# One moving operand of 512 columns for the experts' gate and up matmuls, with the halves added outside TensorE

## The chip, the cores and the metric

The kernel runs on one core of one Trainium2 chip. The metric is the device time of one execution in microseconds. Beside the times there is one profiled execution, and all rows below come from its trace. A core has five engines that run side by side, each through its own queue in order: TensorE (PE in the rows; its weight loads are shown apart as PEld), VectorE (DVE), ScalarE (ACT), GpSimd (POOL) and SyncE (SP), which here only issues transfers.

## The reference

The reference is one block of a diffusion transformer over 2048 tokens of 1024 features: a modulated layer norm, a projection, a gated convolution branch, a retention branch in both directions, a mixing projection, a layer norm, and then a mixture of experts in which each of 16 experts takes its own 256 tokens. The part that matters here is the last:

```
aff = softmax(h @ w_router);  gates, idx = top_k(aff.T, 256)      # per expert
xe  = h[idx]                                                      # 256 x 1024 per expert
he  = silu(xe @ w_gate[e]) * (xe @ w_up[e])                       # 256 x 1024
ye  = (he @ w_down[e]) * gates                                    # 256 x 1024
out = layer_norm(alpha * x + g2 * scatter_add(ye, idx)) * ln2_g + ln2_b
```

## The kernel before, in words

All matrix products run in TensorE's reduced float32 type. To keep float32 accuracy, each operand is split into a high part (the value copied into that type) and a low part (the value minus the high part). A product is then three matmuls into one PSUM bank: high by high, high by low, low by high. The helper `split` (lines 78 to 84) makes the two parts: ScalarE writes the high part (line 80) and VectorE subtracts for the low part (line 81). The helper `mm3` (lines 86 to 89) issues the three matmuls, so lines 87, 88 and 89 stand for all of them in the rows, and lines 80 and 81 for all splits; the tile names tell them apart.

The experts are the loop at line 1160. Per expert:

- `x_gather` (line 1094) fetches the 256 token rows of the next expert by an indirect transfer. `x_prep` (line 1104) transposes them on TensorE and splits them into `xeT`, a tile of 8 blocks of 128 features, in each block first 256 columns of high parts and then 256 of low parts (one column per token).
- Gate and up (lines 1171 to 1181): four steps `f2`, each making two blocks `fb` of 128 hidden features. The weights come in as float32 (`rg`, a ring of 4 buffers, issued by SP) and are split into `sg` tiles (a ring of 24 buffers under the tag `w`, shared with all other split weights and with the row tiles of the end). The weights are the stationary operand, the tokens the moving one. For a block, 8 feature blocks times `mm3` accumulate 256 columns of the gate, then the same for up. One PSUM bank (`pg`) holds the gate of both blocks, one (`pu`) up of both. Then ScalarE applies Silu from the gate's bank (line 1179), VectorE multiplies by the up bank (line 1180), and the product is split into `heT` (line 1181).
- Down (lines 1191 to 1235): two halves `n` of the output features, each 8 steps times two token tiles of `mm3` with 512 moving columns of split `w_down` (`sd`), collected by line 1211 and added into the rows of `d_acc` in memory by an indirect transfer.

PSUM banks for matmuls come from two tags with two buffers each, taken in turn (`mm_ps`, lines 66 to 70), so four banks go round.

The order of the work on each engine is set when the program is built, by a list scheduler that takes instructions by priority (the order of the code) and by its own idea of when they are ready. A block under `issue_after` is held back behind an instruction that it names. The final layer norm of rows is done by `finish` (line 1137), a generator: one step fetches a row tile of 128 tokens, one step `lag` steps later takes its mean and variance and starts the scaling, and the step after that ends it and writes the rows out. `pump` (line 358) runs a given number of such steps at a place in the program. From expert 11 (`FIN`) on, all 16 tiles are finished from `d_acc` as it stands (`fx` tiles); after experts 13 and 14 four tiles each are done again with what the last experts changed (`zr` tiles); the tuple `STEPS` says how many steps are run behind each part of the last two experts. The last expert's own two tiles are finished at the end.

Two small tiles `pad0` and `pad1` (line 951) only move what is allocated behind them. `pad0` has 56 words (224 bytes), after which `heT` starts on a multiple of 128 bytes in its partition. `pad1` has 8 words (32 bytes), after which both `xeT` buffers start 32 bytes past a multiple of 128. The other moving operands of the program (`hT`, the split weights, `SS`) start on a multiple of 128.

Of the kernel before, what the change touches and what calls it, by code (L numbers as in the profile page):

```python
# [20 lines left out]
P = 128  # L21
D = 1024
KD = 8
# [19 lines left out]
def body(ctx: ExitStack, tc: tile.TileContext, x, ctxt, cc, w_ada0, w_ada, b_row, b_col, w_in, conv_w, conv_b,  # L43
# [878 lines left out]
    def e2k(name):  # L922
        return ep.tile([P, 512], F32, name=name, tag="e2k", bufs=6)
# [24 lines left out]
    same, low = ksel[:, 0], ksel[:, 1]  # L948
    wg2 = []
    for i, (tag, bufs) in enumerate((("heT", 1), ("xeT", 2))):  # L950
        V.memset(ep.tile([P, (56, 8)[i]], F32, name=f"pad{i}"), 0.0)
        wg2.append(ep.tile([P, 4, D], F32, name="wg2", tag=tag, bufs=bufs))
        nc.sync.dma_start(wg2[i], w_ada[3, i * 4:i * 4 + 4].rearrange("k p f -> p k f"))
    g2fill = [ada_rows(rep_c(ep)[0], 2, 1, lambda name: e4k(name, [P, 512]), wg2)]
# [197 lines left out]
            yield  # L1152

    FIN = 11
    STEPS = ((1, 1, 1, 1, 1, 0), (1, 1, 1, 2, 1, 0))
    efill = []
    nxt = x_prep(0, x_gather(0))
    make_lists(0)
# [1 line left out]
    for e in range(NE):  # L1160
# [9 lines left out]
        heT = ep.tile([P, KD, 2, 256], F32R, name="heT", tag="heT", bufs=1)  # L1170
        for f2 in range(4):
            wg, wu = first[f2] if e == 0 and f2 < 3 else [gu_slabs(w[e], f2) for w in (w_gate, w_up)]
            pg, pu = mm_ps(), mm_ps()
            for fb in range(2):
                for w, dst in ((wg, pg), (wu, pu)):
                    for k in range(KD):
                        mm3(dst[:, fb * 256:(fb + 1) * 256], w[fb][k], (xeT[:, k, 0], xeT[:, k, 1]), k == 0, k == KD - 1)
            s = e2k("s")
            A.activation(s, pg, AF.Silu)
            evicted = V.tensor_tensor(s, s, pu, ALU.mult)  # L1180
            split(heT[:, f2 * 2:f2 * 2 + 2, 0], heT[:, f2 * 2:f2 * 2 + 2, 1], s.rearrange("p (f c) -> p f c", f=2))
            if f2 == 1 and 1 <= e < 4:
                make_lists(e)
            if f2 == 1 and e + 1 < NE:
                nxt = x_prep(e + 1, xes)
            with tc.issue_after(evicted.ins):
                if e >= NE - 2:
                    pump(STEPS[e - NE + 2][f2], efill)
                elif f2:
                    pump(1 + (f2 == 1), efill)  # L1190
# [45 lines left out]
        if e in (NE - 3, NE - 2):  # L1236

            with tc.issue_after(evicted.ins):
                pump(1000, efill)
                lo = FIN if e == NE - 3 else NE - 3  # L1240
                efill.append(finish(range(lo * 2, lo * 2 + 4), acc_rows, put_rows, 3))
                pump(3 if e == NE - 3 else 2, efill)
        for t in range(2):
            g = e * 2 + t
# [71 lines left out]
```

## Time and profile before

| what | us |
|---|---|
| median of 3 runs | 3033.33 (3030.34 to 3039.99) |
| profiled execution, its own time | 3036.01 |
| its span, first to last instruction | 3034.2 |
| TensorE busy in the span | 2942.8 |
| first gate matmul of expert 0 | 1915.1 |
| one expert in the middle (4 to 12) | 68.3 to 68.4 |
| last down matmul to the end of the span | 14.4 |

The span is read in stages. Everything ahead of the experts takes the first 1915 us; the 16 experts take the rest but for the 14 us at the end. A matmul's row gives the time from its start to its modelled end, and neighbours overlap: what a stream costs is read from start to start. The same holds for VectorE and ScalarE, where the next instruction may start some 0.08 to 0.1 us ahead of the end that a row gives.

### The profile page before, as it was taken

The numbers are of one execution on the slowest core, as the hardware profiler recorded it, in microseconds if no ns is written. First come the engines' busy times: TensorE is split into PE (matmuls) and PEld (weight loads), VectorE is DVE, ScalarE is ACT, GpSimd is POOL, SyncE is SP. The second block draws the span as 40 slices with busy tenths as digits, with TensorE's granted clock in tenths as the row PEclk, the third lists the DMA queues.
The fourth block names the chain that finished last, engine by engine and source line by source line (L and its number), as shares of the span: only waits on it lengthen the run. The fifth ranks groups of instructions, "written<-read, shape, count | busy, mean of one in ns | idle before, by whom it ended". The sixth has DMA issues, their size and how long they took to land.

```text
span 3034.2 us, 47285 instructions
## 1 busy us (share of the span) xinstructions
PE 2942.8 (97%) x18005; PEld 2593.7 (85%) x18005; DVE 2141.6 (71%) x3926; ACT 1160.3 (38%) x2110; POOL 374.7 (12%) x325
## 2 busy tenths in 40 slices
PE   6999999999999999999999996899999999999998
PEld 5988888889888888888878883899999999999997
DVE  4366788552669986888877777666666666668887
ACT  4323223242231333544421112455555555544443
POOL 2100000000000000111101114000000000014332
PEclk9999999999999999999999998899999999999999
DMA  7244345342452334666754445566677776778875
GB/s 252 88 141 174 135 165 183 111 133 93 172 185 81 129 113 143 220 209 209 232 202 153 148 140 185 193 206 210 207 221 219 215 223 214 221 239 279 289 246 205
DMA packets 194853, 559.94 MB, mean 185 GB/s; under 512 B 29017, under 2 KB 44281, under 8 KB 194625
## 3 DMA queue, kind: packets, MB, share of 16 engines
q1 hardware_dynamic: 170080, 486.60, 48.1%
q0 software_dynamic: 18064, 64.62, 7.5%
q10 hardware_dynamic: 6480, 5.70, 0.6%
q8 instruction: 141, 2.31, 0.3%
q14 instruction: 88, 0.71, 0.1%
HBM read 428.95 MB, written 127.89 MB: 184 GB/s over the span
## 4 chain that ended last, share of the span: by engine, by line
PE 87%; DMA 5%; DVE 4%; ACT 2%; issue 2%; POOL 1%; POOLq 0%; SPq 0%; DVEq 0%; ACTq 0%
PE mm L87 24%; PE mm L89 24%; PE mm L88 24%; PE tr L160 2%; PE ro L87 2%; PE ro L89 2%; PE ro L88 2%; DMA rg<-w_up 1%; DVE st L140 1%; PE o L88 1%; PE o L89 1%; PE o L87 1%; DVE sg L81 1%; DMA out<-fx 1%; PE u L160 0%
## 5 line engine op out<-in xcount | busy, mean ns | idle before, releaser
L87 PE MATMUL mm<-xeT,sg 128*128 128x256 f32 x2048 | 574.1, 281 | 0.0
L89 PE MATMUL mm<-xeT,sg 128*128 128x256 f32 x2048 | 572.8, 280 | 1.2 <-DVE sg L81 1.2
L88 PE MATMUL mm<-xeT,sg 128*128 128x256 f32 x2048 | 572.5, 280 | 0.0
L81 DVE TENSOR_TENSOR sg<-rg,sg 128x512 fp32r<-128x512 f32 x488 | 329.5, 689 | 231.8 <-ACT sg L80 229.8
L80 ACT ACTIVATE sg<-rg 128x512 fp32r<-128x512 f32 x512 | 313.6, 629 | 303.1 <-PE mm L89 217.9
L89 PEld LDWEIGHTS mm<-xeT,sg 128*128 128x128 f32 x2048 | 385.6, 188 | 1.6 <-DVE sg L81 1.6
L88 PEld LDWEIGHTS mm<-xeT,sg 128*128 128x128 f32 x2048 | 385.7, 188 | 0.6
L87 PEld LDWEIGHTS mm<-xeT,sg 128*128 128x128 f32 x2048 | 385.5, 188 | 0.6
L491 DVE SCALAR_TENSOR_TENSOR cacc<-yw,cvw,cacc 128x384 f32<-128x384 f32 (+1 forms) x600 | 376.4, 640 | 8.0
L81 DVE TENSOR_TENSOR sd<-rd,sd 128x512 fp32r<-128x512 f32 x256 | 172.0, 688 | 86.8 <-ACT sd L80 86.2
L80 ACT ACTIVATE sd<-rd 128x512 fp32r<-128x512 f32 x256 | 156.9, 629 | 134.7 <-PE mm L89 82.5
L87 PE MATMUL mm<-sd,heT 128*128 128x512 f32 x512 | 199.9, 390 | 1.6 <-ACT heT L80 1.4
L89 PE MATMUL mm<-sd,heT 128*128 128x512 f32 x512 | 199.8, 390 | 0.4 <-DVE heT L81 0.4
L88 PE MATMUL mm<-sd,heT 128*128 128x512 f32 x512 | 199.5, 390 | 0.0
L154 POOL TENSOR_TENSOR rs<-rs,mhalf 128x1 f32<-128x1 f32 (+1 forms) x50 | 38.5, 770 | 1273.3 <-DVE rs L153 1272.8
L87 PE MATMUL mm<-hT,sU 128*128 128x256 f32 x512 | 147.1, 290 | 4.0 <-ACT us L732 2.2
L147 POOL TENSOR_TENSOR rs<-rs,mhalf 128x1 f32<-128x1 f32 x58 | 106.6, 1838 | 345.4 <-DVE rs L146 342.0
L88 PE MATMUL mm<-hT,sU 128*128 128x256 f32 x512 | 147.2, 288 | 0.0
L89 PE MATMUL mm<-hT,sU 128*128 128x256 f32 x512 | 146.6, 288 | 0.0
L1246 POOL DMA_INDIRECT d_acc<-ye,idx x30 | 50.1, 1670 | 567.3 <-DVE ye L1211 470.8
L468 ACT ACTIVATE gs<-mm 128x512 f32<-128x512 f32 x96 | 55.0, 597 | 163.8 <-PE mm L89 142.7
L87 PEld LDWEIGHTS mm<-sd,heT 128*128 128x128 f32 x512 | 96.2, 188 | 21.6 <-ACT heT L80 2.4
(360 smaller groups left out, 7136.4 us busy)
## 6 DMA issues: line engine op xcount, KB each, us to landing
rg<-w_gate SPq DMA_DIRECT2D x128, 512.0 KB, 4.6
rg<-w_up SPq DMA_DIRECT2D x128, 512.0 KB, 3.6
rd<-w_down SPq DMA_DIRECT2D x128, 512.0 KB, 4.3
wa<-w_ada SPq DMA_DIRECT2D x40, 512.0 KB, 4.1
d_v<-vs SPq DMA_DIRECT2D x32, 512.0 KB, 2.6
vsr<-d_v SPq DMA_DIRECT2D x32, 512.0 KB, 5.5
xt<-x SPq DMA_DIRECT2D x16, 512.0 KB, 3.6
rU<-w_in SPq DMA_DIRECT2D x16, 512.0 KB, 4.7
```

Of the source, the lines that this page charges most:

```text
L80: A.activation(hi, src, AF.Copy)
L81: eng.tensor_tensor(lo, src, hi.bitcast(F32), ALU.subtract)
L87: T.matmul(ps, s[0], m[0], start=start, stop=False)
L88: T.matmul(ps, s[0], m[1], start=False, stop=False)
L89: return T.matmul(ps, s[1], m[0], start=False, stop=stop_)
L140: V.bn_stats(st[:, i], src[:, i * w:(i + 1) * w])
L147: pows[0] = G.tensor_tensor(rs, rs, mhalf[:, :1], ALU.pow)
L154: G.tensor_tensor(rs[:, 0], rs[:, 0], mhalf[:, :heads], ALU.pow)
L160: T.transpose(ps[:, j * P:(j + 1) * P], src[:, (k0 + j) * P:(k0 + j + 1) * P], ident)
L468: A.activation(s, ps, AF.Sigmoid)
L491: V.scalar_tensor_tensor(acc[:, :n], y[:, tap:tap + n], cvw[:, cgp, tap:tap + 1], acc[:, :n], op0=ALU.mult, op1=ALU.add)
L1246: G.indirect_dma_start(out=d_acc, out_offset=bass.IndirectOffsetOnAxis(ap=idx[:, g:g + 1], axis=0), in_=yes[t], in_offset=None, compute_op ...
```

## The change

Gate and up no longer use `mm3`. For each weight block and each feature block there are now two matmuls: the high weights against the 512 columns of high and low tokens at once (line 1180 of the new file), and the low weights against the 256 columns of high tokens (line 1181), added into the first half of the same bank. A whole bank now holds one product of one block: the first half has high by high plus low by high, the second half high by low. To end it, ScalarE copies the second half out (line 1182), VectorE adds the first half to the copy (line 1183), and for the gate ScalarE applies Silu in place (line 1185). The multiplication (line 1186) and the split into `heT` are done per block, on 256 columns, where they were done per step on 512.

`pad1` is gone. The finishing generator that is started after expert 14 gets a `lag` of 2 where it had 3, and the last row of `STEPS` is changed.

```diff
     for i, (tag, bufs) in enumerate((("heT", 1), ("xeT", 2))):
-        V.memset(ep.tile([P, (56, 8)[i]], F32, name=f"pad{i}"), 0.0)
+        if i == 0:
+            V.memset(ep.tile([P, 56], F32, name="pad0"), 0.0)
...
-    STEPS = ((1, 1, 1, 1, 1, 0), (1, 1, 1, 2, 1, 0))
+    STEPS = ((1, 1, 1, 1, 1, 0), (1, 1, 2, 1, 0, 0))
...
-            pg, pu = mm_ps(), mm_ps()
             for fb in range(2):
-                for w, dst in ((wg, pg), (wu, pu)):
+                banks = mm_ps(), mm_ps()
+                s = e2k("s")
+                parts = s[:, 0:256], s[:, 256:512]
+                for w, ps, part in zip((wg, wu), banks, parts):
                     for k in range(KD):
-                        mm3(dst[:, fb * 256:(fb + 1) * 256], w[fb][k], (xeT[:, k, 0], xeT[:, k, 1]), k == 0, k == KD - 1)
-            s = e2k("s")
-            A.activation(s, pg, AF.Silu)
-            evicted = V.tensor_tensor(s, s, pu, ALU.mult)
-            split(heT[:, f2 * 2:f2 * 2 + 2, 0], heT[:, f2 * 2:f2 * 2 + 2, 1], s.rearrange("p (f c) -> p f c", f=2))
+                        T.matmul(ps, w[fb][k][0], xeT[:, k].rearrange("p a c -> p (a c)"), start=k == 0, stop=False)
+                        T.matmul(ps[:, 0:256], w[fb][k][1], xeT[:, k, 0], start=False, stop=k == KD - 1)
+                    A.activation(part, ps[:, 256:512], AF.Copy)
+                    V.tensor_tensor(part, part, ps[:, 0:256], ALU.add)
+                    if ps is banks[0]:
+                        A.activation(part, part, AF.Silu)
+                evicted = V.tensor_tensor(parts[0], parts[0], parts[1], ALU.mult)
+                split(heT[:, f2 * 2 + fb, 0], heT[:, f2 * 2 + fb, 1], parts[0])
...
-                efill.append(finish(range(lo * 2, lo * 2 + 4), acc_rows, put_rows, 3))
+                efill.append(finish(range(lo * 2, lo * 2 + 4), acc_rows, put_rows, 3 if e == NE - 3 else 2))
```

ScalarE's queue in an expert in the middle, before, around the end of one step `f2` (`mm` is the gate's bank, `sg` and `sd` are split weights, numbers are buffers):

```order
L80 ACTIVATE sg_23479<-rg_23477 128x512
L80 ACTIVATE sg_23482<-rg_23477 128x512
L80 ACTIVATE sg_23487<-rg_23485 128x512
L1179 ACTIVATE s_23161<-mm_23063 128x512
L80 ACTIVATE sg_23490<-rg_23485 128x512
L80 ACTIVATE sg_23495<-rg_23493 128x512
L80 ACTIVATE sg_23498<-rg_23493 128x512
L80 ACTIVATE heT_23030<-s_23161 128x2x256
```

And now, for one block `fb`, half a step:

```order
L1182 ACTIVATE s_21223<-mm_21221 128x256
L80 ACTIVATE sg_21581<-rg_21576 128x512
L1185 ACTIVATE s_21223<-s_21223 128x256
L80 ACTIVATE sg_21586<-rg_21584 128x512
L1182 ACTIVATE s_21223<-mm_21222 128x256
L80 ACTIVATE sg_21589<-rg_21584 128x512
L80 ACTIVATE heT_21188<-s_21223 128x256
```

The weight splits keep their order; between each two of them now stands an instruction of 256 columns that belongs to a bank, and the Silu stands behind an addition on VectorE.

VectorE's queue at the same places, before:

```order
L81 TENSOR_TENSOR sg_23487<-rg_23485,sg_23487 128x512
L81 TENSOR_TENSOR sg_23490<-rg_23485,sg_23490 128x512
L81 TENSOR_TENSOR sg_23495<-rg_23493,sg_23495 128x512
L1180 TENSOR_TENSOR s_23161<-s_23161,mm_23064 128x512
L81 TENSOR_TENSOR sg_23498<-rg_23493,sg_23498 128x512
L81 TENSOR_TENSOR heT_23030<-s_23161,heT_23030 128x2x256
```

and now:

```order
L1183 TENSOR_TENSOR s_21223<-s_21223,mm_21221 128x256
L81 TENSOR_TENSOR sg_21581<-rg_21576,sg_21581 128x512
L81 TENSOR_TENSOR sg_21586<-rg_21584,sg_21586 128x512
L1183 TENSOR_TENSOR s_21223<-s_21223,mm_21222 128x256
L1186 TENSOR_TENSOR s_21223<-s_21223 128x256
L81 TENSOR_TENSOR sg_21589<-rg_21584,sg_21589 128x512
L81 TENSOR_TENSOR heT_21188<-s_21223,heT_21188 128x256
```

Where a step of 16 weight splits had two instructions of 512 columns, it now has eight of 256.

VectorE's queue in the last expert, at the end of gate and up and into down, before (`zr` are row tiles being finished, line 1211 collects the first half of down):

```order
L1180 TENSOR_TENSOR s_29858<-s_29858,mm_29761 128x512
L1146 SCALAR_TENSOR_TENSOR zr_29290<-zr_29290,rs1_29724,l2_26027 128x1024
L81 TENSOR_TENSOR heT_29298<-s_29858,heT_29298 128x2x256
L140 BN_STATS st_29865<-zr_29434 128x6 x2
L140 BN_STATS st_29876<-zr_29571 128x6
L143 BN_AGGR mv_29868<-st_29865 128x2
L140 BN_STATS st_29876<-zr_29571 128x6
L146 TENSOR_SCALAR rs1_29870<-mv_29868 128x1
L1151 SCALAR_TENSOR_TENSOR zr_29434<-zr_29434,mv_29868,l2_26026 128x1024
L143 BN_AGGR mv_29879<-st_29876 128x2
L1146 SCALAR_TENSOR_TENSOR zr_29434<-zr_29434,rs1_29870,l2_26027 128x1024
```

and now:

```order
L1183 TENSOR_TENSOR s_28754<-s_28754,mm_28753 128x256
L81 TENSOR_TENSOR heT_28276<-s_28711,heT_28276 128x256
L1186 TENSOR_TENSOR s_28754<-s_28754 128x256
L1147 SCALAR_TENSOR_TENSOR zr_28524<-zr_28524,rs1_28673,l2_25277 128x1024
L81 TENSOR_TENSOR heT_28276<-s_28754,heT_28276 128x256
L81 TENSOR_TENSOR sd_28822<-rd_28817,sd_28822 128x512
L81 TENSOR_TENSOR sd_28827<-rd_28825,sd_28827 128x512
```

The finishing of the last two repeated row tiles, which stood behind the last `heT`, now stands ahead of it; behind it are weight splits for down.

## Rows read from the trace of the kernel before

**Rows 1.** The page: busy us, share of the span and instructions of each engine.
```profile
PE 2942.8 (97%) x18005; PEld 2593.7 (85%) x18005; DVE 2141.6 (71%) x3926; ACT 1160.3 (38%) x2110; POOL 374.7 (12%) x325
```

**Rows 2.** Windows: busy us (instructions) per engine, TensorE's clock, DMA share, GB/s.
```profile
2469.80:2538.10 68.30, 68.30 (x497) 64.56 (x496) 43.30 (x65) 36.97 (x62) 5.14 (x4) 1.00 0.70 216
...
2743.20:2811.50 68.30, 68.30 (x497) 64.58 (x496) 57.33 (x94) 32.53 (x60) 29.34 (x22) 1.00 0.85 286
2811.50:2881.90 70.40, 68.96 (x498) 64.47 (x497) 60.38 (x100) 30.14 (x57) 25.55 (x22) 1.00 0.86 288
2881.90:2950.50 68.60, 68.60 (x498) 64.64 (x497) 56.30 (x89) 33.57 (x62) 25.39 (x17) 1.00 0.78 256
2950.50:3019.80 69.30, 67.58 (x481) 62.55 (x479) 55.98 (x91) 26.76 (x48) 18.44 (x14) 1.00 0.67 228
```

**Rows 3.** What TensorE waited for in the experts: us in total, times, longest.
```profile
PE mm L87 <- ACT heT L80: 1.4, 1, 1.4
PE mm L89 <- DVE sg L81: 1.2, 1, 1.2
PE ix L1048 <- ACT ob L1047: 1.2, 3, 0.4
PE mm L89 <- DVE heT L81: 0.4, 1, 0.4
```

**Rows 4.** Page, groups: xcount | busy us, mean ns of one | idle before.
```profile
L87 PE MATMUL mm<-xeT,sg 128*128 128x256 f32 x2048 | 574.1, 281 | 0.0
```

**Rows 5.** Timeline of TensorE, gate and up of expert 5: start us, us, what.
```profile
2299.74 0.28 PE L87 MATMUL mm<-xeT,sg 128*128 128x256 f32 x1
...
2300.09 0.28 PE L87 MATMUL mm<-xeT,sg 128*128 128x256 f32 x1
2300.09 0.19 PEld L88 LDWEIGHTS mm<-xeT,sg 128*128 128x128 f32 x1
...
2306.27 0.28 PE L89 MATMUL mm<-xeT,sg 128*128 128x256 f32 x1
```

**Rows 6.** Timeline of TensorE, down of expert 5.
```profile
2319.72 0.39 PE L88 MATMUL mm<-sd,heT 128*128 128x512 f32 x1
...
2329.92 0.39 PE L88 MATMUL mm<-sd,heT 128*128 128x512 f32 x1
```

**Rows 7.** Timeline of TensorE, the first projection.
```profile
719.78 0.28 PE L89 MATMUL mm<-hT,sU 128*128 128x256 f32 x1
...
726.98 0.28 PE L89 MATMUL mm<-hT,sU 128*128 128x256 f32 x1
```

**Rows 8.** Timeline of VectorE: four instructions of 256 columns and the next.
```profile
2074.81 0.42 DVE L1041 TENSOR_TENSOR oa<-pabf,kio 128x256 fp32r<-128x256 f32 x1
...
2076.15 0.69 DVE L81 TENSOR_TENSOR sd<-rd,sd 128x512 fp32r<-128x512 f32 x1
```

**Rows 9.** Timeline of VectorE, expert 13.
```profile
2857.00 4.29 DVE L81 TENSOR_TENSOR sd<-rd,sd 128x512 fp32r<-128x512 f32 x7
...
2867.84 0.69 DVE L81 TENSOR_TENSOR heT<-s,heT 128x512 fp32r<-128x512 f32 x1 [3.41 <-ACT heT L80]
```

**Rows 10.** Timeline of ScalarE, expert 8.
```profile
2478.38 0.60 ACT L1179 ACTIVATE s<-mm 128x512 f32<-128x512 f32 x1 [0.77 <-PE mm L89]
```

**Rows 11.** Groups by line, ScalarE with 256 columns: xcount | busy us, mean ns | idle before.
```profile
L680 ACT ACTIVATE o<-o,rs 128x256 f32<-128x256 f32 x64 | 30.9, 564 | 43.3 <-DVE rs L155 43.3
```

**Rows 12.** What ScalarE waited for from expert 11 on: us in total, times, longest.
```profile
ACT sd L80 <- DMA rd<-w_down: 34.4, 19, 4.2
...
ACT sd L80 <- DMA out<-fx: 11.1, 2, 7.5
```

**Rows 13.** Groups within 2743.2 to 2811.5 (expert 12), VectorE.
```profile
L1146 DVE SCALAR_TENSOR_TENSOR fx<-fx,rs,l 128x1024 f32<-128x1024 f32 x6 | 7.7, 1278 | 0.0
```

## Prediction

> **What bounds the kernel now.** I read the page first: TensorE is busy 97% of the span and VectorE 71% [rows 1]. A share over the whole span says little here, so the second view is the busy time in windows, one per expert [rows 2]. The reader is to see two things. In the middle (first line) TensorE is busy for all of 68.3 us and VectorE for 43.3, ScalarE for 37.0: TensorE alone sets the pace. In the last four experts VectorE is at 57.3, 60.4, 56.3 and 56.0 us, since the row tiles are finished there, and two windows are longer: 70.4 and 69.3. The third view, what TensorE waited for, has only some 4 us in all sixteen experts [rows 3]. So time can only be won by fewer or shorter matmuls, and can be lost where VectorE or ScalarE come late, which is near in the last four experts and far in the others.
>
> What a matmul costs is read in the timeline from start to start, since the 281 ns of the group [rows 4] overlap. In gate and up, 57 matmuls start between 2299.74 and 2306.27, so 56 steps of 116.6 ns [rows 5]. In down, with 512 columns, 45 steps from 2319.72 to 2329.92 are 226.7 ns each [rows 6]. In the first projection, 256 columns again, 60 steps take 7.20 us, 120.0 ns each [rows 7]. Between 256 and 512 columns lie 106.7 ns (226.7 less 120.0), which is 256 columns at the upper level of 2.4 GHz, and the granted clock is 1.00 in these windows [rows 2]. So every matmul costs its columns and something on top: 13.3 ns in down and in the first projection, 10 ns in gate and up. What differs between these places and is set by the program is where the moving tile starts: on a multiple of 128 bytes in the two with 13.3, and 32 bytes past one in gate and up.
>
> **The change, part by part.**
>
> *The matmuls.* Gate and up have 2048 triples (16 experts, 4 steps, 2 blocks, 2 weights, 8 feature blocks). A triple is 768 columns before and after; three instructions become two. Before: 3 x 116.6 = 349.9 ns. With the small pad gone, the token tile starts on a multiple of 128 like the moving tiles of rows 6 and 7, so I take their steps: 226.7 + 120.0 = 346.7 ns. That is 3.2 ns for 2048 triples: 6.6 us less. The bounds are wider. If the 10 ns of gate and up stay with both instructions, a triple is 116.6 + 106.7 + 116.6 = 339.9 ns, 20.5 us less. If the first instruction carries the 13.3 and the other columns run no better than the slowest 256-column step plus the same again, 226.7 + 124 (120.0 with the 4 ns that the rows scatter by), the triple is 351 and the change costs 2 us. I take the middle, because the rows with the tile's new placement say so in two stages.
>
> The Trainium skill has a formula for this gap in "TensorE: Matmul & The Clock Gate", section "Back-to-back issue gap": columns at 2.4 GHz plus 2.5 ns. By it one instruction less per triple would bring 2.5 x 2048 = 5.1 us; the rows show four to five times as much on top of the columns, but only the part that is not given back by the placement counts.
>
> *The eviction in the experts before 11.* Per expert VectorE loses 8 instructions of 512 columns and gains 32 of 256 (16 additions, 8 multiplications, 8 subtractions). From start to start, 512 columns take 0.60 us (seven in 4.29, less the last one's 0.69, over 6) [rows 9] and 256 take 0.335 (four in 1.34) [rows 8]. So 32 x 0.335 - 8 x 0.60 = 5.9 us more, 43.3 to 49.2 of 68. ScalarE loses 8 of 512 (0.60 each) [rows 10] and gains 32 of 256, each at most 0.56 [rows 11]: at most 13 us more, 37.0 to 50. Both stay hidden behind TensorE. What could uncover them is a bank that comes free late. Four banks go round; a bank is filled in 8 x 0.347 = 2.8 us, and three others are filled before it is needed again: 8.3 us. After the last matmul the Silu started 0.77 us later [rows 10]; with that wait, a copy of at most 0.56, an addition of 0.42 and one weight split ahead on each engine (0.63 and 0.69), a bank is free after 3.1 us. That is 5 us in hand, where before a pair had 11.2 us (four blocks of 2.8) for its eviction. Cost in these experts: nothing. The last `heT` block is first needed in the seventh of eight steps of down, 36 matmuls of 227 ns or 8.2 us on; nothing either.
>
> *The last four experts.* VectorE's busy time there is 57.3 + 60.4 + 56.3 + 56.0 = 230.0 of 276.6 us [rows 2]. The change adds 4 x 5.9 = 23.7: 253.7 us, 92%. Its idle time halves, 46.6 to about 21. A finishing instruction of 1024 columns holds its queue 1.28 us [rows 13] and the additions that free a bank stand behind such ones; ScalarE's copies stand behind weight splits that wait for rows to be written out (7.5 us once, on which VectorE then sat idle 3.41) [rows 12, 9]. Now the price. With TensorE alone, expert 13 would take 68.3 like the middle, and expert 15, which has no transposes, 384 x 0.1166 + 96 x 0.2267 = 66.6; so these windows hold 2.1 + 0.3 + 2.7 = 5.1 us of stalls today. Below, the new stalls can be nothing: the waits on writes come from the same places with the same lead. Above, VectorE sets the pace and keeps all its idle time: 23.7 us more, less the 1.7 that these experts would have won. I take 4 us more: the same waits on half the idle time.
>
> *The lag of 2 and STEPS.* The order shows that in the last expert the two-tile finishing work that stood between the last `heT` and down now stands ahead of it. It can give back at most the 2.7 us of expert 15 and lose none of its work, which is the same; a tile waits one step less for its reciprocal root from GpSimd, which is behind by then. I take 1 us. The pad's memset itself is one instruction far from any wait: nothing.
>
> **Sum.** 6.6 less for the matmuls, 4 more and 1 less at the end: 3.6 us less than the profiled execution's own 3036.0, so 3032.4. The median of the runs shown is 2.7 us below that execution, so I expect 3029.7, and say 3029. About 0.3% (9.1 us) is what a measurement of this kernel can tell from no change; the forecast is inside it.
>
> **The rivals.**
>
> *A. The smaller step on top of the columns holds for the new pair.* The stationary tiles are the same, and the 10 ns belong to gate and up in 6144 matmuls; if it is these weights and not the token tile's place that make them, the triple is 339.9 ns. Against it: both other stages have 13.3. Time: 20.5 less, 3 back at the end: 17.5 less, 3016.
>
> *B. VectorE becomes the bound in the last four experts (slower).* For it: 92% busy in a queue in strict order, with finishing instructions of 1.28 us ahead of the additions that free TensorE's banks, and only 8.3 us for a bank where it was 11.2. Against it: at 84 to 86% it cost 5 us in three windows. It decides when an addition comes more than 8.3 us after its bank's last matmul. Price 23.7 in full, less the 6.6 won on all matmuls: 17 more, 3050.
>
> *C. The eviction paces gate and up everywhere (slower).* Each gate bank now goes ScalarE, VectorE, ScalarE, and each hop stands behind a weight split. If a hop on average waits for two splits and not one, 3.1 us grow by 2.6 to 5.7, still under 8.3; only with four ahead does it break. Were it to cost 0.15 us a bank, 256 banks would be 38 us: 3065. Against it: ScalarE and VectorE have 18 us to spare per expert.
>
> *D. Weight loads are the bound.* PEld is busy 64.6 of 68.3 us in the middle [rows 2], and a third of gate and up's loads go. Then all that stands on top of the columns could vanish: a triple of 768 columns at 320 ns, 30 less, 61 us in all, 2972. Against it: a load starts with the matmul ahead of it (both at 2300.09) [rows 5], takes 0.19 us, and has 0.227 behind a matmul of 512 columns, yet that stream shows 13.3 on top too.
>
> The Trainium skill's "Perfetto Trace Analysis", section "Identifying the Most-Contended Engine", would have TensorE's headroom judged by the loads' busy share, which here is 94%; it is the page behind D, and rows 5 and 6 disagree with it for this stream.
>
> **How the numbers follow.** Chances: forecast 0.56, A 0.24, B 0.12, C 0.04, D 0.04. The forecast's own range, from bounds on stalls and scatter, is 3020 to 3038; 0.2 of it lies beyond 9.1 us faster, little beyond 9.1 slower. Faster by over 0.3%: 0.11 of the forecast's, 0.21 of A, 0.04 of D, together 0.36. Slower by over 0.3%: 0.03 of the forecast's, 0.10 of B, 0.04 of C, 0.17. Within: 0.47. The range of 8 in 10 takes in A and the lower half of B: 3010 to 3044.
>
> **What would show it.** In the changed trace, starts in gate and up should lie 227 and 120 ns apart in turn; 223 and 117 is A, much less is D. An expert in the middle should take 67.9 us with TensorE waiting for nothing; a wait of the new first matmul (line 1180) for line 1183's addition would be C in the middle and B after expert 11. VectorE should be busy near 49 us in the middle and 60 to 66 per window at the end, with TensorE's waits there 6 to 12 us in all. The forecast is wrong if the pair takes under 342 or over 350 ns, or if the last four experts together take over 282 us.

## The result, and the profile after

The changed kernel took 3059.14 us (median of 5 runs, 3052.51 to 3060.61), the kernel before 3032.82 beside it: ratio 1.0081, with an interval of 1.0065 to 1.0097. That is 26 us slower where 4 us less were forecast. The profiled execution took 3058.51, 22.5 us more than that of before. The stretch ahead of the experts is the same work in all runs of this document, but for a pad, and yet took between 1906 and 1918 us from one profiled execution to the next (one of the eighteen, a slow one at about half clock, is left out), so the rows per expert tell more than a single time: from the first gate matmul to the end of the span the changed kernel took 1145.5 us and that of before 1119.1, 26.4 more.

First where the time went. Windows of the changed kernel, one per expert; columns as in [rows 2] (length, busy us of TensorE, its loads, VectorE, ScalarE and GpSimd, then TensorE's clock, DMA share, GB/s). The first is expert 8, the others are experts 12 to 15:

```profile
2467.10:2535.50 68.40, 68.40 (x370) 58.99 (x369) 50.00 (x89) 42.48 (x86) 5.29 (x4) 1.00 0.72 216
2740.90:2809.40 68.50, 68.50 (x369) 58.86 (x368) 61.65 (x114) 34.23 (x76) 21.98 (x22) 1.00 0.79 268
2809.40:2890.00 80.60, 73.32 (x370) 62.02 (x369) 68.45 (x126) 39.69 (x86) 25.00 (x23) 0.94 0.76 258
2890.00:2967.60 77.60, 71.71 (x369) 61.11 (x368) 62.16 (x114) 40.28 (x86) 20.40 (x16) 0.93 0.74 236
2967.60:3045.60 78.00, 69.49 (x353) 58.10 (x352) 65.11 (x121) 33.91 (x74) 20.32 (x15) 0.98 0.63 206
```

An expert in the middle takes what it took; everything is lost in the last three: 236.2 us against 208.3 [rows 2], 27.9 more. (The experts started 3.9 us earlier in this execution, which is why the whole differs by 22.5; the first thirteen took 1.8 more, the tail behind the last matmul 3.2 less.) The 27.9 have two parts. TensorE's idle time there, length less busy, is 21.7 us against 3.2: 18.5 more. And it is busy for 214.5 us with matmuls that took 205.1: 9.4 more, at a granted clock of 0.94, 0.93 and 0.98 where it was 1.00.

What TensorE waited for from expert 12 on (us in total, times, longest), against [rows 3]:

```profile
PE mm L1180 <- DVE s L1183: 11.6, 4, 3.7
PE mm L1180 <- ACT sg L80: 5.9, 1, 5.9
PE mm L87 <- DVE s L1183: 2.8, 2, 2.0
```

The first and third are the new addition (line 1183), which frees a bank. The second is a wait for a weight split on ScalarE; it comes third in time below.

Each long wait costs twice. The clock in expert 13, in stretches around two such waits:

```profile
2838.00:2842.00 4.00, 4.00 (x25) 3.48 (x24) 1.64 (x4) 0.49 (x2) 0.00 (x0) 1.00 1.01 400
2842.00:2845.50 3.50, 0.80 (x5) 0.43 (x4) 1.41 (x3) 2.23 (x5) 0.00 (x0) 1.00 1.02 410
2845.50:2852.30 6.80, 5.49 (x16) 4.31 (x16) 6.80 (x12) 5.51 (x13) 0.55 (x1) 0.50 0.61 224
2852.30:2855.70 3.40, 0.27 (x1) 0.27 (x2) 3.34 (x9) 1.16 (x3) 1.47 (x1) 1.00 0.38 154
2855.70:2859.10 3.40, 3.40 (x12) 2.85 (x12) 3.40 (x7) 2.39 (x7) 1.36 (x2) 0.50 0.29 118
```

and TensorE's own rows behind the first:

```profile
2846.46 0.80 PE L1180 MATMUL mm<-xeT,sg 128*128 128x512 f32 x1 [3.66 <-DVE s L1183]
...
2847.27 0.63 PE L1180 MATMUL mm<-xeT,sg 128*128 128x512 f32 x1
...
2847.91 0.63 PE L1180 MATMUL mm<-xeT,sg 128*128 128x512 f32 x1
```

TensorE idled for 3.66 us up to 2846.46. Near the end of that wait the clock fell to 0.50 (1.2 and not 2.4 GHz), and a pair took 0.64 us where it takes 0.35. Near 2852.3 it rose again, while TensorE idled for the second time (3.47 us, up to 2855.43), and fell once more for 3.4 us behind that wait. The wait of 1.4 us that the kernel before had in expert 13 left the clock at 1.00 [rows 2, 3].

Why the addition was late both times, in VectorE's rows:

```profile
2842.87 1.29 DVE L81 TENSOR_TENSOR sg<-rg,sg 128x512 fp32r<-128x512 f32 x2 [3.23 <-ACT sg L80]
2845.39 0.69 DVE L81 TENSOR_TENSOR sg<-rg,sg 128x512 fp32r<-128x512 f32 x1 [1.22 <-ACT sg L80]
2845.99 0.41 DVE L1183 TENSOR_TENSOR s<-s,mm 128x256 f32<-128x256 f32 x1
...
2849.99 1.28 DVE L1147 SCALAR_TENSOR_TENSOR fx<-fx,rs,l 128x1024 f32<-128x1024 f32 x1
2851.19 1.87 DVE L140 BATCH_NORM_STATS2 st<-fx 128x6 f32<-128x512 f32 x3
...
2855.01 0.37 DVE L1183 TENSOR_TENSOR s<-s,mm 128x256 f32<-128x256 f32 x1
```

The first addition stands behind three weight splits, which wait for ScalarE's half of the split. ScalarE in turn waited for a slab that had not landed:

```profile
2842.21 1.15 ACT L80 ACTIVATE sg<-rg 128x512 fp32r<-128x512 f32 x2 [3.71 <-DMA rg<-w_up]
```

Why that slab came late no run settles. The second addition, at 2855.01, stands behind 5 us of row finishing. The third long wait, in expert 14, is of yet another kind. VectorE's finishing instruction itself waits for GpSimd's root. The next addition and the multiplication stand behind it, ScalarE's copy into `heT` waits for the multiplication, and the weight splits that TensorE needs next stand behind that copy:

```profile
2903.87 1.28 DVE L1147 SCALAR_TENSOR_TENSOR fx<-fx,rs,l 128x1024 f32<-128x1024 f32 x1 [4.31 <-POOL rs L147]
2905.07 0.41 DVE L1183 TENSOR_TENSOR s<-s,mm 128x256 f32<-128x256 f32 x1
...
2906.04 0.42 ACT L80 ACTIVATE heT<-s 128x256 fp32r<-128x256 f32 x1 [7.26 <-DVE s L1186]
...
2907.30 0.80 PE L1180 MATMUL mm<-xeT,sg 128*128 128x512 f32 x1 [5.89 <-ACT sg L80]
```

This is no wait for a bank: TensorE had filled four blocks of expert 14, and the first of their banks had been freed by an addition at 2897.66. So there are three blockers (a late slab, a row being finished, GpSimd's root) and two ways to TensorE, both through a queue in strict order: the addition that frees its bank stands behind something that is waiting or long, or its next weights stand behind an eviction that does.

Now the matmuls. TensorE's timeline in expert 6, first a stretch ahead of the transposes of the next expert's tokens, then one behind them; between the two rows of each lie 30 pairs:

```profile
2336.73 0.40 PE L1180 MATMUL mm<-xeT,sg 128*128 128x512 f32 x1
...
2347.33 0.40 PE L1180 MATMUL mm<-xeT,sg 128*128 128x512 f32 x1
...
2356.81 0.39 PE L1180 MATMUL mm<-xeT,sg 128*128 128x512 f32 x1
...
2367.21 0.39 PE L1180 MATMUL mm<-xeT,sg 128*128 128x512 f32 x1
```

A pair takes 353.3 ns in the first stretch and 346.7 in the second. Both stretches read the same token tile in the same shapes. Most experts have one of each kind, 350.0 in the mean, which is the triple of before; experts 3, 7 and 9 have 353.2 throughout. The change wins nothing on matmuls here.

### The profile page after: what moved, and what is told of

Read it like the earlier page. It is cut to its first block, busy times and chain, and to the rows that moved or that the text cites. A ratio compares the mean times of both kernels' runs of the same rounds, so it can differ in the third digit from the quotient of the medians.

```text
span 3056.7 us, 43677 instructions
## 1 busy us (share of the span) xinstructions
PE 2953.2 (97%) x15957; PEld 2507.5 (82%) x15957; DVE 2243.9 (73%) x4309; ACT 1251.5 (41%) x2494; POOL 358.0 (12%) x325
## 4 chain that ended last, share of the span: by engine, by line
PE 86%; DMA 5%; DVE 4%; issue 2%; ACT 2%; POOL 1%; POOLq 0%; SPq 0%; DVEq 0%; ACTq 0%
PE mm L87 18%; PE mm L88 18%; PE mm L89 18%; PE mm L1180 12%; PE mm L1181 6%; PE tr L160 2%; PE ro L87 2%; PE ro L89 2%; PE ro L88 2%; DMA rg<-w_up 1%; DVE st L140 1%; PE o L87 1%; PE o L89 1%; PE o L88 1%; DVE sg L81 1%
## 5 line engine op out<-in xcount | busy, mean ns | idle before, releaser
L1180 PE MATMUL mm<-xeT,sg 128*128 128x512 f32 x2048 | 731.5, 400 | 17.9 <-DVE s L1183 11.6
L1181 PE MATMUL mm<-xeT,sg 128*128 128x256 f32 x2048 | 578.9, 283 | 1.2 <-DVE sg L81 1.2
L1180 PEld LDWEIGHTS mm<-xeT,sg 128*128 128x128 f32 x2048 | 388.1, 190 | 110.9 <-DVE s L1183 13.7
L1181 PEld LDWEIGHTS mm<-xeT,sg 128*128 128x128 f32 x2048 | 390.8, 191 | 3.0 <-DVE sg L81 2.1
L1183 DVE TENSOR_TENSOR s<-s,mm 128x256 f32<-128x256 f32 x256 | 106.5, 418 | 79.0 <-ACT s L1182 78.6
L1182 ACT ACTIVATE s<-mm 128x256 f32<-128x256 f32 x256 | 97.2, 380 | 127.6 <-PE mm L1181 125.0
L147 POOL TENSOR_TENSOR rs<-rs,mhalf 128x1 f32<-128x1 f32 x58 | 86.2, 1486 | 332.2 <-DVE rs L146 332.1
L87 PEld LDWEIGHTS mm<-sd,heT 128*128 128x128 f32 x512 | 96.1, 188 | 23.7 <-DVE s L1183 3.5
```

The lines of the kernel that those rows point to most:

```text
L87: T.matmul(ps, s[0], m[0], start=start, stop=False)
L147: pows[0] = G.tensor_tensor(rs, rs, mhalf[:, :1], ALU.pow)
L1180: T.matmul(ps, w[fb][k][0], xeT[:, k].rearrange("p a c -> p (a c)"), start=k == 0, stop=False)
L1181: T.matmul(ps[:, 0:256], w[fb][k][1], xeT[:, k, 0], start=False, stop=k == KD - 1)
L1182: A.activation(part, ps[:, 256:512], AF.Copy)
L1183: V.tensor_tensor(part, part, ps[:, 0:256], ALU.add)
```

## The experiments

Ratios are to the kernel before, run on the same chip.

**The token tile's place.** The changed kernel with the pad back, and the kernel before without it:

```diff
-        if i == 0:
-            V.memset(ep.tile([P, 56], F32, name="pad0"), 0.0)
+        V.memset(ep.tile([P, (56, 8)[i]], F32, name=f"pad{i}"), 0.0)
```

> The changed kernel with the 32-byte pad put back, so that the token tiles start 32 bytes past a multiple of 128, as before the change. Theory P (the prediction's): the token tile's place sets what stands on top of the columns, 10 ns here and 13.3 on a multiple of 128. Then a pair of matmuls takes 340 ns where the changed kernel shows 350 in most experts and 353.2 in four, and the kernel is 2048 x 10 to 13 ns faster than the changed one: 3032 to 3039. Rival R: the stage pays 14 ns per 256 columns whatever the place (350 ns per 768 columns before and after alike); the pair stays at 350 to 353 and the kernel at 3055 to 3063. The stalls of the last three experts stay in both.

Measured: 3055.12, ratio 1.0063 [1.0042, 1.0083]. The pair took neither 340 nor 350 but 346.8 ns in every expert. TensorE's timeline in expert 6, two rows that follow each other and one 30 pairs behind the first:

```profile
2336.72 0.39 PE L1179 MATMUL mm<-xeT,sg 128*128 128x512 f32 x1
2336.95 0.28 PE L1180 MATMUL mm<-xeT,sg 128*128 128x256 f32 x1
...
2347.12 0.39 PE L1179 MATMUL mm<-xeT,sg 128*128 128x512 f32 x1
```

10.40 us for 30 pairs; experts 4 to 11 took 67.92 us each, the figure that the forecast named, but with the pad and not without it. The stalls of the last three experts stayed (241.7 us for the three), so the time came out at theory R's lower edge although the pair was neither theory's.

> The kernel before without the 32-byte pad: the token tiles start on a multiple of 128 bytes, everything else is as before. Theory P: three matmuls take 3 x 120.0 = 360 ns where they took 350, 2048 x 10 = 20 us more: 3053. Rival R: 350 ns as before, 3030 to 3037.

Measured: 3049.55, ratio 1.0054 [1.0038, 1.0070]; a triple took 360.0 ns in all experts. So the place counts, as theory P has it, and for three matmuls by the forecast's 10 ns. The whole grew by 16 us and not by 20, since experts 13 to 15 took 208.7 us where they had taken 208.3: at the longer step TensorE idled there for 1.2 us in place of 3.2. Two more places:

> The hybrid (changed matmuls in experts 0 to 10, three matmuls in 11 to 15) with one token buffer 64 and the other 96 bytes past a multiple of 128, for the steps of TensorE alone: experts alternate between the buffers. If only a start on a multiple of 128 is dear, both show 346.8 ns a pair and 350.0 a triple, as 32 bytes past does. If the place counts in finer steps, one of them shows 340 (10 ns on top of the columns for each of two) or 350 to 353.

Measured (one run, 3033.32): in the even experts a pair takes 350.1 ns and a triple 360.0; in the odd ones a pair takes 348.9 ahead of the transposes and mostly 353.4 behind them (351.1 in the mean), and a triple 353.4. The trace doesn't show which of the two buffers is the one 64 bytes past and which the one 96 past. Thirty-two bytes past is the best of the four places for both in the mean, and there the pair is 3.2 ns ahead of the triple.

**Parts that cost nothing.** Half steps alone, with three matmuls per block:

```diff
-            pg, pu = mm_ps(), mm_ps()
             for fb in range(2):
+                pg, pu = mm_ps(), mm_ps()
+                s = e2k("s")[:, 0:256]
...
+                A.activation(s, pg[:, 0:256], AF.Silu)
+                evicted = V.tensor_tensor(s, s, pu[:, 0:256], ALU.mult)
```

> The kernel before with its three matmuls and the pad, but with the changed kernel's banks: one bank per block of gate or up (256 of its 512 columns used), Silu, multiplication and split per block on 256 columns; no copy and no addition. A bank is refilled 8.3 us after its last matmul and not 11.2; VectorE has 0.6 us more per expert. Theory C (the shorter cover alone costs): stalls in experts 13 to 15 as in the changed kernel, 3046 to 3056. Theory H (what costs is that a bank is freed only after a copy on ScalarE and an addition on VectorE that waits for it, each behind splits that wait for something): 3030 to 3038, since up's bank needs VectorE alone and gate's ScalarE alone.

Measured: 3032.37, ratio 0.9988 [0.9977, 0.9998]. Banks turning round in 8.3 us instead of 11.2, and eviction in halves, cost nothing by themselves. Theory C falls.

Lag and STEPS as before:

```diff
-    STEPS = ((1, 1, 1, 1, 1, 0), (1, 1, 2, 1, 0, 0))
+    STEPS = ((1, 1, 1, 1, 1, 0), (1, 1, 1, 2, 1, 0))
...
-                efill.append(finish(range(lo * 2, lo * 2 + 4), acc_rows, put_rows, 3 if e == NE - 3 else 2))
+                efill.append(finish(range(lo * 2, lo * 2 + 4), acc_rows, put_rows, 3))
```

> The changed kernel with the lag of 3 and the last row of STEPS as before. By the prediction these are worth 1 us for the change, so 3060. If they do more, the last expert's 78 us (69.4 before) come down: to 3050 to 3055 if the finishing tiles ahead of the last block are what makes its wait.

Measured: 3059.64, ratio 1.0082 [1.0068, 1.0096]. Expert 15 took 74.9 us there and 77.9 with the new row, the tail 14.4 and 11.2: what one gives the other takes.

Writes of finished rows cut to one row of 128, in both places that write them:

```diff
-        G.dma_start(out[t * P:(t + 1) * P], z)
+        G.dma_start(out[t * P:t * P + 1], z[0:1])
...
```

> The changed kernel with the finishing arithmetic, but each finished tile of 128 rows writes one row and not 128 (the last expert's own two tiles are written whole), so that 24 writes of 512 KB go. Theory T: weight slabs land earlier and the stalls of the last three experts go: 3031 to 3040. Theory L: VectorE's work is the same and the stalls stay: 3050 to 3060.

Measured: 3057.94, ratio 1.0077 [1.0056, 1.0097]. The stalls stayed, so the writes beside the slabs are not their cause.

**VectorE's load alone.** In the kernel before, 16 instructions of 256 columns per expert that nothing reads:

```diff
+                    V.tensor_tensor(ksel.rearrange("p a c -> p (a c)"), ksel.rearrange("p a c -> p (a c)"), ksel.rearrange("p a c -> p (a c)"), ALU.mult)
```

> The kernel before with 16 more VectorE instructions of 256 columns per expert, each on a scratch tile that nothing reads, one behind each block's gate and each block's up; matmuls, banks and eviction as before. This is the load of the change's 16 additions (16 x 0.335 = 5.4 us per expert) without its place in the way of a bank. Theory L: the load is what costs, 20 to 27 us more: 3053 to 3060. Theory Q: the banks are still freed with 11.2 us in hand and nothing hangs on the additions: 0 to 7 us more, 3032 to 3040.

This missed its aim: with no data to wait for, they were all put into the first four experts (in experts 0 to 2 VectorE's rows add up to 75 to 80 us each, where they had 43 to 48), and the last experts had none. Its 3043.53 (1.0024 [1.0009, 1.0039]) says nothing on the last three experts. It does show what load alone costs where nothing is finished beside it: VectorE was busy for 94 to 98% of experts 0 to 2, and they took 219.6 us against 210.8, 3 us each. Held behind each step's multiplication (`issue_after`):

> The kernel before with 16 VectorE instructions of 256 columns per expert on a scratch tile that nothing reads, four behind each multiplication that ends a step of gate and up, held there in the order (in the run before this one they had drifted into the first experts). Matmuls, banks and eviction as before. Theory L: 5.4 us of VectorE time per expert is what costs in the last three experts: TensorE stalls there and drops its clock, 3050 to 3060. Theory Q: only the additions' place between a bank's last matmul and its reuse costs; this load hides: 3030 to 3040.

Measured: 3045.18, ratio 1.0041 [1.0026, 1.0057], 12 us. Windows of experts 13 to 15 of this kernel, then TensorE's waits from expert 12 on:

```profile
2804.70:2876.70 72.00, 69.23 (x498) 64.27 (x497) 65.00 (x114) 31.65 (x58) 24.74 (x23) 1.00 0.82 275
2876.70:2949.40 72.70, 69.36 (x498) 64.85 (x497) 64.55 (x111) 34.63 (x64) 22.23 (x17) 1.00 0.81 263
2949.40:3021.80 72.40, 69.14 (x481) 63.67 (x479) 62.01 (x110) 28.51 (x51) 17.59 (x15) 0.98 0.64 221
```

```profile
PE mm L89 <- DVE sg L81: 4.6, 4, 2.1
PE mm L88 <- DVE sd L81: 2.4, 2, 2.2
```

VectorE is about as busy as in the changed kernel (191.6 us in three experts against 195.7), yet the three take 217.1 us and not 236.2, 8.8 more than in the kernel before. (This profiled execution, 3037.14, is the fastest of six, because its experts began 7.1 us earlier than those of before; the rows per expert don't depend on that.) The waits are for weights and not for banks, none is over 2.2 us, and in two of the three windows the clock stays at 1.00. Load is part of the cause and not the whole of it.

**The banks and their two hops.** Six banks for gate and up from expert 4 on:

```diff
-                banks = mm_ps(), mm_ps()
+                banks = (gu_ps(), gu_ps()) if e >= 4 else (mm_ps(), mm_ps())
...
-                ps = tr_ps() if e < 4 or t == 0 else u_ps("tr2")
+                ps = tr_ps()
```

> The changed kernel, but from expert 4 on gate and up take six PSUM banks in turn and not four (the token transposes then use two banks and not four), so that a bank has 5 x 2.8 = 14 us to be emptied where it had 8.3. Theory Q: TensorE stalls in the last three experts because the copy and the addition that free its bank stand behind weight splits whose transfer has not landed, and behind finishing instructions; with 14 us the 21 us that TensorE waited there and the time at the lower clock behind each wait shrink to a few us: 3033 to 3042. Theory L: VectorE has not the time for 16 more additions per expert while it finishes rows; more banks do not give it time: 3053 to 3062.

Measured: 3068.91, ratio 1.0108 [1.0071, 1.0144], worse. What TensorE waited for:

```profile
PE tr L166 <- DVE xeT L87: 17.2, 5, 8.1
PE mm L1186 <- ACT sg L86: 6.0, 1, 6.0
PE mm L93 <- DVE s L1189: 4.9, 1, 4.9
```

No wait in gate and up is put down to the addition (now line 1189) any more; down's first matmul waits for it once, for 4.9 us. The same late queue now holds the transposes, which had lost two banks to make six, and experts 11 and 12 lose time too (75.2 and 72.3 us). So the run doesn't confirm Q, and doesn't refute it cleanly either: it moved the shortage of banks from one user to another.

Without the hop over ScalarE:

```diff
-                    A.activation(part, ps[:, 256:512], AF.Copy)
-                    V.tensor_tensor(part, part, ps[:, 0:256], ALU.add)
+                    V.tensor_reduce(part, ps.rearrange("p (a c) -> p c a", a=2), axis=AX.X, op=ALU.add)
```

> The changed kernel with the two halves of a bank added by one VectorE reduction over pairs of columns (512 read, 256 written), so that ScalarE's copy is gone and VectorE alone frees a bank. VectorE's load grows by some 0.27 us x 16 = 4 us per expert, ScalarE's falls by 6 us. Theory H: the hop over ScalarE's queue is what makes the waits for a bank, and they shrink to under 6 us; the load's own cost stays: 3040 to 3050. Theory L: more load, more stalls: 3062 to 3080.

Measured: 3071.01, ratio 1.0107 [1.0087, 1.0127]. What TensorE waited for:

```profile
PE mm L1181 <- DVE sg L81: 13.9, 10, 2.5
PE mm L88 <- DVE sd L81: 4.6, 4, 3.5
PE mm L1180 <- DVE s L1182: 3.9, 3, 1.9
PE mm L87 <- DVE s L1182: 2.7, 2, 2.5
```

Waits for banks fell from 14.4 to 6.6 us, nearly as H has it (under 6), but waits for weight splits rose from 1.2 to 18.5, and the time is L's: with another 4 us per expert on VectorE the split weights themselves come late.

**Without the finishing arithmetic**, in both kernels:

```diff
-                V.scalar_tensor_tensor(xs[u], xs[u], rs[u], l2[1], op0=ALU.mult, op1=ALU.add)
...
-                rs[u], mv = ln_scale(xs[u], 2, eps=EPS / ALPHA ** 2, fin=False)
-                V.scalar_tensor_tensor(xs[u], xs[u], mv[:, 0, 0:1], l2[0], op0=ALU.subtract, op1=ALU.mult)
```

> The changed kernel without the arithmetic of the finishing steps (statistics, scaling; VectorE's and GpSimd's), except that of the last expert's own two tiles; the rows are fetched and written out as they are, so the transfers stay. Theory L: VectorE has 13 us and more per expert free again and the stalls go: 3059 less 22 to 28, 3031 to 3037. Theory T (the transfers: weight slabs land late because rows are read and written beside them, and the queues stand behind their splits): the stalls stay, 3050 to 3060.

Measured: 3076.56, ratio 1.0141 [1.0121, 1.0161].

> The kernel before without the arithmetic of the finishing steps (as in the changed kernel's run without it, which took 3077 and whose VectorE was busy for under 52 us of 76 to 84). Both run the same transfers with VectorE far from full; only matmuls, banks and eviction differ. Theory H (a copy that stands on ScalarE behind a split that waits for a row tile's write holds a bank, whatever VectorE's load): here no bank hangs on such a copy, so 3020 to 3040, and some 35 to 55 us less than the changed kernel without arithmetic. If instead leaving the arithmetic out is what does the harm (rows fetched and written at other times), it does it here too: 3055 to 3080.

Measured: 3075.26, ratio 1.0148 [1.0131, 1.0165]. The edit harms both alike, so it doesn't tell L and H apart, and the first of the two alone says nothing on the change. What ScalarE waited for from expert 11 on, in the kernel before without arithmetic:

```profile
ACT sd L80 <- DMA out<-fx: 31.9, 5, 8.3
ACT sg L80 <- DMA out<-zr,idx: 29.8, 5, 12.6
ACT sg L80 <- DMA out<-fx: 28.8, 4, 9.0
```

against 11.1 and 5.0 us for the `fx` rows in the kernel before itself. A weight split that takes over a row tile's buffer waits until the row is written out, and everything behind it on ScalarE waits too. Why these waits grow when the arithmetic goes was not tested.

**As much load away as the change adds.** The two scaling instructions of a finishing step on half the columns, with all transfers and waits in place, in the changed kernel and in that of before:

```diff
-                V.scalar_tensor_tensor(xs[u], xs[u], rs[u], l2[1], op0=ALU.mult, op1=ALU.add)
+                V.scalar_tensor_tensor(xs[u][:, 0:512], xs[u][:, 0:512], rs[u], l2[1][:, 0:512], op0=ALU.mult, op1=ALU.add)
...
```

> The changed kernel with the two scaling instructions of each finishing step on 512 of the 1024 columns (the statistics, GpSimd's part, all transfers and waits stay; half of each finished row is left unscaled). VectorE has some 1.2 us less per row tile, 6 to 7 us per expert from the twelfth on, a little more than the change added. Theory L (VectorE's load is what costs): most of the 26 us go, 3033 to 3042. Theory H (the bank's two hops behind other work cost by themselves): the waits for the addition stay, 3048 to 3060.

Measured: 3042.22, ratio 1.0033 [1.0020, 1.0046]. TensorE's waits from expert 12 on, then the windows of experts 13 to 15:

```profile
PE mm L1180 <- DVE s L1183: 4.0, 3, 2.2
PE mm L87 <- DVE s L1183: 3.8, 4, 2.4
```

```profile
2806.50:2877.60 71.10, 68.91 (x369) 58.84 (x368) 62.37 (x125) 37.11 (x82) 20.73 (x23) 1.00 0.85 290
2877.60:2946.00 68.40, 68.40 (x370) 58.93 (x368) 55.00 (x112) 38.93 (x86) 17.05 (x16) 1.00 0.77 253
2946.00:3025.10 79.10, 72.63 (x353) 59.95 (x351) 60.93 (x121) 32.42 (x73) 18.33 (x15) 0.94 0.59 200
```

Experts 13 and 14 take 139.5 us together, where the kernel before took 139.0 [rows 2]: with about that kernel's load on VectorE (117.4 against 116.7 us) the two-step eviction costs them almost nothing. What is left lies in the last expert, 79.1 us against 69.3, where VectorE is still busy for 5 us more than before (60.9 against 56.0). One of its two long waits for a bank, 2.2 us, is plainly the hop over ScalarE. VectorE had nothing to do for 3.45 us because the copy stood behind weight splits whose slab was late:

```profile
2972.89 1.15 ACT L80 ACTIVATE sg<-rg 128x512 fp32r<-128x512 f32 x2 [3.40 <-DMA rg<-w_gate]
...
2974.34 0.42 DVE L1183 TENSOR_TENSOR s<-s,mm 128x256 f32<-128x256 f32 x1 [3.45 <-ACT s L1182]
```

The other, 2.4 us, has its addition behind row finishing.

> The same edit in the kernel before, as the control: VectorE there has 6 to 7 us less per expert at the end. By both theories it takes away at most the 5 us of stalls of experts 13 to 15: 3027 to 3035. If it is much above, the edit does harm by the order that it changes, and the run beside it says nothing.

Measured: 3029.15, ratio 0.9983 [0.9970, 0.9996], so the edit as a whole does no harm by itself (it does move waits: expert 14 took 74.5 us, the other two 68.3 and 68.2). It takes 0.48% (1.0081 less 1.0033, 15 us) off the changed kernel and 0.17% (5 us) off that of before. The time lies at the upper end of theory L's range, and the changed kernel stays 0.50% above the control: at a lighter load the addition still holds banks for 7.8 us.

**A version without the loss.** The pair, with the pad, where no rows are finished beside it:

```diff
+            if e < FIN:
+                for fb in range(2):
+                    banks = mm_ps(), mm_ps()
...
+            else:
+                pg, pu = mm_ps(), mm_ps()
```

> The kernel before, pad and last steps as before, with the changed matmuls and eviction in experts 0 to 10 alone; experts 11 to 15, beside which rows are finished, keep three matmuls and the eviction of 512 columns. From the changed kernel with the pad (346.8 ns a pair against 350.0 ns a triple) each of these eleven experts should take 0.4 us less, 4.6 us in all, and the last five what they took before: 3028. If an eviction of the new kind slows even the experts beside which nothing is finished: 3033 to 3040.

Measured: 3028.15, ratio 0.9986 [0.9975, 0.9997], 4 us less, as worked out. With the pair up to expert 11 and half steps from 12 on:

> A version that should beat both: pad as before, the pair of matmuls with its additions in experts 0 to 11, and in experts 12 to 15, beside which rows are finished, three matmuls with one bank per block of gate and of up (as in the run on half steps). By the two runs on these parts (ratios 0.9986 and 0.9988) 3.5 to 8 us less than before: 3025 to 3030. If the order of experts 12 to 15 comes out worse behind the pairs, 3030 to 3038.

Measured: 3028.20, ratio 0.9978 [0.9967, 0.9990], by which it is 6.7 us faster than the kernel before, and so faster than both. Its experts 12 and 13 took 68.4 and 68.3 us; 14 and 15, at full clock too:

```profile
2875.50:2944.70 69.20, 68.67 (x497) 64.64 (x496) 57.34 (x99) 34.22 (x70) 20.28 (x17) 1.00 0.77 258
2944.70:3014.40 69.70, 67.66 (x481) 62.94 (x479) 58.86 (x104) 27.16 (x56) 18.00 (x15) 1.00 0.65 227
```

## Why the prediction was wrong, point by point

*What bounds the kernel.* Right: TensorE in the middle, and room to lose only in the last four experts.

*The matmuls, 6.6 us less.* Wrong: nothing was won. The step "the token tile starts on a multiple of 128 like the moving tiles of rows 6 and 7, so I take their steps" was half right. That the place counts was shown twice (360 ns for a triple without the pad; 346.8 for a pair with it). But two steps from streams of one shape each do not add up to the step of a stream that alternates: on a multiple of 128 the pair falls into one of two patterns, 346.7 or 353.3, and the mean is the old 350. The first of them equals the forecast's sum, and so does the pair 32 bytes past, where theory P gave 340; no run says why, so that agreement can't be counted for the sum. Rival A's 340 appeared at none of the four places. Rival D is gone too: without a third of gate and up's loads, the loads' busy time in a middle expert fell from 64.6 of 68.3 us to 59.0 of 68.4, and the expert took as long. The Trainium skill's "Perfetto Trace Analysis", section "Identifying the Most-Contended Engine", would judge TensorE's headroom by its share of peak arithmetic or by the loads' busy share; the second of these doesn't hold for this stream, by the same two numbers.

*The eviction up to expert 10, nothing.* Right: 68.40 us with TensorE busy throughout; VectorE 50.0 (49.2 forecast), ScalarE 42.5 (at most 50). One term was misread: the 0.77 us of rows 10 is ScalarE's idle time ahead of the Silu, which started 0.04 us after the end of the matmul that it waited for. The 3.1 us until a bank is free were thus too long by some 0.7, which changes nothing.

*The last four experts, 4 us more, at most 22.* This is the step that failed, in size and in its upper bound. The mechanism was rival B's, named with its place (the addition behind finishing work) but with a chance of 0.12: "VectorE's idle time halves, 46.6 to about 21", and "the same waits on half the idle time". The last three experts lost 27.9 us. VectorE did not become the bound in B's sense, busy throughout: it worked for 195.7 of their 236.2 us. (B's 84 to 86% are of experts 12 and 13; the three windows that it means had 81 to 86%.) Three things were missing from the sum. Load alone costs more than I took: 12 us in the run that adds nothing else, with VectorE then busy for 88% of those windows. The two-step eviction turns lateness into waits of 3.5 us and more, for a bank behind a late slab and behind a row tile, and for weights behind GpSimd's root. And behind such waits TensorE runs at 1.2 GHz for a time: 9.4 us, more than the 6.6 that the change was to win on matmuls. The bound of 23.7 less 1.7 counted VectorE's work alone and left waiting and the clock out, so it was no bound.

*How it divides.* That the copies and additions beside the finishing of rows make the loss is shown by elimination. Banks and eviction by halves cost nothing with three matmuls (half steps), the pair takes no longer than the triple, the pad is worth a few us, lag and STEPS nothing, and the pair with its copies and additions costs nothing in experts 0 to 11. How the 26 us divide is shown only in part. Load by itself makes 12 us (8 to 17 by its interval); taking about as much away wins back 15 of the 26. The 10 us that are then left over the kernel before lie in the last expert, where VectorE still has more to do than before and where this run has the new lag and STEPS, which its control has not. That the hop over ScalarE and the place behind finishing work make this rest is read from the trace. No run put the copies and additions into the kernel before without their load, and none added ScalarE's copies alone, so this stays argued; and the parts need not add, since one can lengthen the other.

*Lag and STEPS, 1 us less.* Nothing, within 1.0082 and 1.0081; expert 15 loses the 3 us that the tail gains.

*Rival C* was rightly small: no wait for a bank before expert 13.

## What to carry to other kernels

Taking instructions from the busiest engine and giving their work to others paid here only where those had slack and where nothing that TensorE waits for stood behind their other duties: use the new form in the stages with slack and keep the old one elsewhere, and judge it per stage. Price a wait of TensorE by its length: in these runs waits of 1 to 2 us mostly cost what they lasted, and those of 3.5 us and more their length and a stretch at half clock; in between both were seen. And when a step time is carried over from another stream, carry it for the same sequence of shapes and the same start of the tile, not shape by shape.

## What the runs showed of the hardware that I had not expected

- The start of the moving tile changes a matmul's step, and a start on a multiple of 128 bytes is not the best. For pairs (512 and 256 columns) and triples (three of 256): 0 bytes past a multiple of 128, 346.7 or 353.3 ns and 360.0; 32 past, 346.8 and 350.0; of 64 and 96 past, one has 350.1 and 360.0 and the other 348.9 or 353.4 and 353.4.
- On a multiple of 128 the same stream of pairs keeps one of two steps (353.3 or 346.7) for 20 us and more, and in most experts changes it where the transposes interrupt it (expert 6: 353.3 ahead of them, 346.7 behind). Triples 32 bytes past do it too, rarely: 353.3 in place of 350.0 in two stretches of the run with the load in place and in one of that on half steps.
- Leaving out all finishing arithmetic made both kernels slower, the changed one by 1.4% and that of before by 1.5%. In the latter ScalarE's splits then waited 90.5 us from expert 11 on for buffers of rows still being written; that these waits are the cause is read from the trace and not tested.
